# A decoder block on one core: the key numbers as sixteen steps, and most of the choice's conversions on ScalarE

## The chip, the cores and the metric

The kernel runs on one core of a Trainium2 chip. The metric is the device time of one execution in microseconds (us); the median of several runs is compared. The engines are named as the profile names them: PE is TensorE's matrix unit, PEld its weight loads, ACT is ScalarE, DVE is VectorE, POOL is GpSimd, and SP is the engine that issues most transfers.

## The reference, cut to what matters

The block mixes 512 tokens (an RWKV group and a sliding-window attention group) and then passes them through a channel mixer that retrieves experts by product keys. Only this last part touches the change. Each of 8 heads scores a token against two sets of 128 subkeys; the 16 best of each set are kept, their sums are ranked, the 16 best pairs are chosen, and each pair names one of 16384 experts:

```python
q = (x_b @ wq).reshape(-1, H, 2, PEER_HALF)
s = jnp.einsum('thcd,hcnd->thcn', q, subkeys)
s_top, i_top = lax.top_k(s, K)                       # K = 16
cand_s = s_top[:, :, 0, :, None] + s_top[:, :, 1, None, :]
cand_i = i_top[:, :, 0, :, None] * 128 + i_top[:, :, 1, None, :]
best_s, best_pos = lax.top_k(cand_s.reshape(-1, H, K * K), K)
idx = jnp.take_along_axis(cand_i.reshape(-1, H, K * K), best_pos, axis=-1)
gate = jax.nn.softmax(best_s, axis=-1)
u = u_tab[idx]
act = gelu(einsum('td,ted->te', x_b, u))
y = einsum('te,ted->td', gate * act, v_tab[idx])
```

## The kernel before

After the mixers the program has three stages that matter here. In the **selection stage** a loop (`for hc in range(16)`) makes the scores of one half-head a pass and ranks them. In the **gate stage** that follows, DVE builds one-hot tables of the chosen experts, PE multiplies them into a dense table of gates, and POOL gathers rows for 128 tokens. In the **main loop** over 128 blocks of experts PE does the dense products.

One pass of the selection loop is called a slot here, by its `hc` (slot 4, slot 5, ...). The order on each engine is the order of the code, since the whole stage is scheduled by hand (`manual_schedule` over POOL, DVE, ACT, PE and SP). A slot issues:

- `wq_split(hc + 1)`: ACT rounds the next slot's projection weights (`wqh`, L166), POOL makes their remainder (`wql`, L167);
- PE: the query product `pq` (24 matmuls, L176 to L178; every third one uses `wql`), and ACT copies it to `q`;
- two steps of work ahead for the main loop (`ups`): ACT rounds expert weights (`uh`), POOL makes `ul` (DVE does so for the later blocks), PE multiplies them (`pA`), ACT applies GELU (`act`);
- one step of the pending choice (`todo`);
- PE: the scores `psc` from `q` and the subkeys; ACT copies them to `sc`; DVE ranks them (`top`: five groups of MAX8, FIND_INDEX8 and MATCH_REPLACE8);
- one more step of the pending choice.

After four slots a set of eight (head, token tile) rows is ranked, and `choose` is started for it; its steps are spread over the next four slots. With the slots counted from the start of a set's choice (4, 5, 6, 7 for the first set):

- slot 4, first step: `fi` (the key numbers as floats), their differences `df` and the candidate sums `cand` on POOL; second step: DVE ranks half of `cand`;
- slot 5, second step: DVE ranks the other half into `bp`, then `ex`, `pf` (the positions as floats) and the first pair of comparisons `ge` against the offsets of the 16 candidate rows;
- slot 6, first step: POOL multiplies the pair `ge` by `df`; second step: DVE sums them into `ro`, adds the first key number, converts and splits the position (`bp`, `rn`, `ro`, `pf`), and makes the second pair `ge`;
- slot 7, first step: POOL multiplies that pair; second step: DVE sums it, ACT takes the exponential of `ex`, and the results go to `sg_`.

Three sets run so (`h0` of 0, 2 and 4, slots 4 to 15). The fourth (`h0 == 6`) runs after the loop with all its arithmetic on DVE, beside products ahead on PE, and the gate stage starts from its results.

Of the kernel before, what the change touches and what calls it, by code (L numbers as in the profile page):

```python
# [7 lines left out]
F32 = mybir.dt.float32  # L8
# [5 lines left out]
OP = mybir.AluOpType  # L14
# [8 lines left out]
TOPK = 16  # L23
# [31 lines left out]
OFFS = [sum(NCAND[:a]) for a in range(16)]  # L55
# [15 lines left out]
def peer_block_kernel(tc, A, out, dbg=None, stop=None):  # L71
    with ExitStack() as ctx:
        _emit(ctx, tc, A, out, dbg or {}, stop)


def _emit(ctx, tc, A, out, dbg, stop):
    nc = tc.nc
    V, SC, PE, GP, SY = nc.vector, nc.scalar, nc.tensor, nc.gpsimd, nc.sync
# [57 lines left out]
    for lv in range(5):  # L136
        b = 1 << lv
        n = 32 // (2 * b)
        for q in range(4):
# [6 lines left out]
                             base=0, channel_multiplier=1)  # L146
            GP.affine_select(out=m[:, :, b:2 * b], in_=m[:, :, b:2 * b],
                             pattern=[[2 * b, n], [0, b]], compare_op=OP.is_ge, fill=0.0,
                             base=b - 1, channel_multiplier=-1)
# [632 lines left out]
    iota = mp.tile([128, 128], F32, name="iota")  # L782
# [212 lines left out]
    sg_ = selp.tile([128, 3, NT, 8, TOPK], F32, name="sg_")  # L995
    tk = tkst.enter_context(tc.tile_pool(name="tk", bufs=1, side="right", reuse_waits="tile"))
    subk = tk.tile([128, 16, 128], F32, name="subk")
    SY.dma_start(subk, A["subk"])

    offs = tk.tile([128, 2, 15], F32, name="offs")  # L1000
    for a in range(1, 16):
        GP.memset(offs[:, 0, a - 1:a], float(OFFS[a]))
        GP.memset(offs[:, 1, a - 1:a], 128.0 * (OFFS[a] - OFFS[a - 1]))
    B815 = [128, 4, TOPK, 15]

    def top(rows):

        for v_, _, x in rows:
            V.max(v_[:, 0:8], x)
        for v_, i_, x in rows:  # L1010
            V.max_index(i_[:, 0:8], v_[:, 0:8], x)
        for v_, _, x in rows:
            V.match_replace(x, v_[:, 0:8], x, LOWEST)
        for v_, _, x in rows:
            V.max(v_[:, 8:16], x)
        for v_, i_, x in rows:
            V.max_index(i_[:, 8:16], v_[:, 8:16], x)

    def choose(h0, tv, ti):

        E_ = GP if h0 < 6 else V
        fi = tk.tile([128, 2, 8, TOPK], F32, name="fi", tag="fi", bufs=2)
        V.tensor_copy(fi, ti)
        df = tk.tile([128, 2, 8, 15], F32, name="df", tag="df", bufs=2)
        E_.tensor_tensor(out=df, in0=fi[:, :, :, 1:16], in1=fi[:, :, :, 0:15], op=OP.subtract)
        E_.tensor_tensor(out=df[:, 0], in0=df[:, 0], in1=offs[:, 1, None, :].to_broadcast([128, 8, 15]), op=OP.add)
        cand = tk.tile([128, 8, NC_], F32, name="cand", tag="cand", bufs=2)
        s1, s2 = tv[:, 0], tv[:, 1]
        for a in range(8):
            n = NCAND[a]  # L1030
            E_.tensor_tensor(out=cand[:, :, OFFS[a]:OFFS[a] + n], in0=s1[:, :, a:a + 1].to_broadcast([128, 8, n]),
                             in1=s2[:, :, 0:n], op=OP.add)
        E_.tensor_tensor(out=cand[:, :, OFFS[8]:], in0=s1[:, :, 8:16], in1=s2[:, :, 0:1].to_broadcast([128, 8, 8]),
                         op=OP.add)
        yield
        bv_ = tk.tile([128, 8, TOPK], F32, name="bv", tag="bv", bufs=2)
        bp = tk.tile([128, 8, TOPK], U32, name="bp", tag="bp", bufs=2)
        for hh in range(2):
            top([(bv_[:, g], bp[:, g], cand[:, g, :]) for g in range(4 * hh, 4 * hh + 4)])
            if hh == 0:  # L1040
                yield
                yield

        gs = tk.tile([128, 8], F32, name="gs", tag="gs", bufs=2)
        ex = tk.tile([128, 8, TOPK], F32, name="ex", tag="ex", bufs=2)
        V.tensor_tensor(out=ex, in0=bv_, in1=bv_[:, :, 0:1].to_broadcast([128, 8, TOPK]), op=OP.subtract)

        if h0 == 6:
            SC.activation(ex, ex, AF.Exp)
        pf = tk.tile([128, 8, TOPK], F32, name="pf", tag="pf", bufs=2)  # L1050
        V.tensor_copy(pf, bp)
        ro = tk.tile([128, 8, TOPK], F32, name="ro", tag="ro", bufs=2)
        rn = tk.tile([128, 8, TOPK], U32, name="rn", tag="rn", bufs=2)

        def pick(src, steps, base, dst):

            ges = []
            for hh in range(2):
                hs = slice(4 * hh, 4 * hh + 4)
                ge = tk.tile(B815, F32, name="ge", tag="ge", bufs=2)  # L1060
                V.tensor_tensor(out=ge, in0=src[:, hs, :, None].to_broadcast(B815),
                                in1=steps[:, None, None, :].to_broadcast(B815), op=OP.is_ge)
                ges.append(ge)
            yield
            for hh in range(2):
                hs = slice(4 * hh, 4 * hh + 4)
                E_.tensor_tensor(out=ges[hh], in0=ges[hh],
                                                    in1=df[:, base, hs, None, :].to_broadcast(B815), op=OP.mult)
            yield
            for hh in range(2):  # L1070
                hs = slice(4 * hh, 4 * hh + 4)
                V.tensor_reduce(dst(hh), ges[hh], axis=AX.X, op=OP.add)
                V.tensor_tensor(out=dst(hh), in0=dst(hh), in1=fi[:, base, hs, 0:1].to_broadcast([128, 4, TOPK]),
                                op=OP.add)


        yield from pick(pf, offs[:, 0, :], 0, lambda hh: ro[:, 4 * hh:4 * hh + 4])
        V.tensor_copy(bp, ro)
        V.tensor_scalar(rn, bp, 7, None, op0=OP.logical_shift_right)
        V.tensor_scalar(bp, bp, 127, None, op0=OP.bitwise_and)  # L1080
        V.tensor_copy(ro, rn)
        V.tensor_tensor(out=pf, in0=pf, in1=ro, op=OP.subtract)
        yield from pick(pf, iota[:, 1:16], 1, lambda hh: sg_[:, 2, :, h0 + hh, :])
        if h0 < 6:
            SC.activation(ex, ex, AF.Exp)
        HT = [128, 2, NT, TOPK]

        def by_tile(i):
            return sg_[:, i, :, h0:h0 + 2, :].rearrange("p t h s -> p h t s")

        def by_head(x):
            return x.rearrange("p (h t) s -> p h t s", t=NT)

        V.tensor_copy(by_tile(1), by_head(bp))
        V.tensor_reduce(gs, ex, axis=AX.X, op=OP.add)
        V.reciprocal(gs, gs)
        V.tensor_tensor(out=by_tile(0), in0=by_head(ex),
                        in1=gs.rearrange("p (h t) -> p h t", t=NT)[:, :, :, None].to_broadcast(HT), op=OP.mult)
# [12 lines left out]
    for hc in range(16):  # L1111
        h_, c_h = hc // 2, hc % 2
        if hc % 4 == 0:
            tv = tk.tile([128, 2, 8, TOPK], F32, name="tv", tag="tv", bufs=2)
            ti = tk.tile([128, 2, 8, TOPK], U32, name="ti", tag="ti", bufs=2)
# [25 lines left out]
        if hc % 4 == 3:  # L1141
            todo = choose(h_ - 1, tv, ti)
# [17 lines left out]
    tk = tkst.enter_context(tc.tile_pool(name="oh", bufs=1, side="right", reuse_waits="tile"))  # L1160
# [327 lines left out]
```

## Time and profile before

| | us |
|---|---|
| median of 3 runs | 1629.78 (1628.6 to 1633.54) |
| the profiled execution | 1630.73, of which span 1629.0 |
| PE busy | 1572.6 (97%) |
| DVE busy | 1286.1 (79%) |
| ACT busy | 652.5 (40%) |
| POOL busy | 742.4 (46%) |

The shares are means over stages with different limits, so the stage around the change has to be read by itself. The selection stage with the fourth set lies between about 374 and 579 us of the span, the gate stage between 579 and about 840 us. What a stage costs is read from which engine waits there, and for whom.

### The profile page before, as it was taken

The page shows a single profiled execution, that of the slowest core. Times are in us where ns is not written, and L with a number is a line of the kernel's source. Part 1 is how long each engine was busy: PE and PEld are TensorE (multiplying, and loading weights), DVE is VectorE, ACT ScalarE, POOL GpSimd, SP SyncE. Part 2 cuts the span into 40 slices and gives each one's busy share as a digit, 9 for nine tenths or more (in the row PEclk, how much of TensorE's full clock was granted, in tenths as well). Part 3 has the DMA queues.
Part 4 walks back from the last instruction along what each step waited for, and adds up shares of the span by engine and source line. Part 5 has one row for each costly group of instructions (what it writes and reads, how often), then busy time and mean ns, then how long its engine had stood idle before and what let it go on. Part 6 is the DMA issues. An engine that isn't in the chain of part 4 may idle for free.

```text
span 1629.0 us, 30768 instructions
## 1 busy us (share of the span) xinstructions
PE 1572.6 (97%) x11869; PEld 1366.7 (84%) x11869; DVE 1286.1 (79%) x2497; ACT 652.5 (40%) x1092; POOL 742.4 (46%) x711
## 2 busy tenths in 40 slices
PE   7999999899999889999999999999999999999997
PEld 4777777797999888888988888888888888888886
DVE  6666567756899999999677788777878877887896
ACT  5333345544444344454433333333333333333334
POOL 5121123244676512222155555555655556556582
PEclk9999999999999999999999999999999999999999
DMA  4111110333232269999999888889998988989793
GB/s 143 53 42 42 59 48 2 129 124 103 79 104 91 98 214 336 348 323 354 320 345 351 304 309 320 322 299 316 331 308 301 333 312 303 321 303 339 236 311 136
DMA packets 180548, 371.18 MB, mean 228 GB/s; under 512 B 17840, under 2 KB 102320, under 8 KB 180144
## 3 DMA queue, kind: packets, MB, share of 16 engines
q1 hardware_dynamic: 137488, 226.71, 40.6%
q0 software_dynamic: 36864, 134.23, 22.9%
q10 hardware_dynamic: 6048, 8.26, 1.4%
q8 instruction: 93, 1.52, 0.4%
q14 instruction: 55, 0.45, 0.1%
HBM read 333.62 MB, written 35.52 MB: 227 GB/s over the span
## 4 chain that ended last, share of the span: by engine, by line
PE 50%; DVE 11%; DMA 3%; issue 1%; ACT 1%; POOL 1%; SPq 0%; DVEq 0%; ACTq 0%
PE acc L1359 10%; PE acc L1358 10%; PE acc L1357 10%; PE pA L178 7%; PE pA L176 7%; PE pA L177 7%; DVE O L1228 3%; DVE ul L167 2%; DVE scr L1182 2%; DVE P L1233 2%; DMA u<-in_uT_dram 2%; DMA row<-in_vB_dram,ix 1%; DMA v<-in_vB_dram 0%; PE pG L1255 0%; POOL row L1169 0%
## 5 line engine op out<-in xcount | busy, mean ns | idle before, releaser
L178 PE MATMUL pA<-h2hi,ul 128*128 128x384 f32 x1024 | 346.2, 338 | 9.9 <-DVE ul L167 5.6
L176 PE MATMUL pA<-h2hi,uh 128*128 128x384 f32 x1024 | 350.3, 342 | 1.5 <-ACT actd L969 1.5
L177 PE MATMUL pA<-h2lo,uh 128*128 128x384 f32 x1024 | 344.1, 336 | 0.0
L1169 POOL DMA_INDIRECT row<-in_u_dram,ix x128 | 175.2, 1369 | 285.7 <-DVE scr L1182 247.7
L1359 PE MATMUL acc<-vl,wh 128*128 128x512 f32 x768 | 300.3, 391 | 1.5 <-DVE vl L167 1.5
L1358 PE MATMUL acc<-vh,wl 128*128 128x512 f32 x768 | 300.0, 391 | 0.2 <-DVE wl L167 0.2
L1357 PE MATMUL acc<-vh,wh 128*128 128x512 f32 x768 | 298.9, 389 | 1.3 <-ACT vh L166 1.3
L1169 POOL DMA_INDIRECT row<-in_vB_dram,ix x128 | 196.1, 1532 | 141.1 <-DVE x L1180 115.7
L167 DVE TENSOR_TENSOR vl<-v,vh 128x1024 fp32r<-128x1024 f32 x128 | 213.9, 1672 | 35.2 <-ACT vh L166 34.4
L178 PEld LDWEIGHTS pA<-h2hi,ul 128*128 128x128 f32 x1024 | 192.8, 188 | 14.8 <-DVE ul L167 10.5
L176 PEld LDWEIGHTS pA<-h2hi,uh 128*128 128x128 f32 x1024 | 193.0, 188 | 4.7 <-ACT actd L969 1.6
L177 PEld LDWEIGHTS pA<-h2lo,uh 128*128 128x128 f32 x1024 | 193.2, 189 | 3.0
L1180 DVE SCALAR_TENSOR_TENSOR x<-row,ac,x 128x1024 f32<-128x1024 f32 x128 | 173.2, 1353 | 7.9 <-DMA row<-in_vB_dram,ix 6.0
L1359 PEld LDWEIGHTS acc<-vl,wh 128*128 128x128 f32 x768 | 144.1, 188 | 32.2 <-DVE vl L167 2.2
L1357 PEld LDWEIGHTS acc<-vh,wh 128*128 128x128 f32 x768 | 144.2, 188 | 30.0 <-ACT vh L166 1.6
L1358 PEld LDWEIGHTS acc<-vh,wl 128*128 128x128 f32 x768 | 144.1, 188 | 29.4 <-DVE wl L167 0.6
L1182 DVE SCALAR_TENSOR_TENSOR scr<-row,h2g 128x1024 f32<-128x1024 f32 x128 | 158.2, 1236 | 1.3
L166 ACT CAST uh<-u 128x1024 fp32r<-128x1024 f32 x128 | 133.9, 1046 | 62.2 <-PE pA L177 29.5
L167 DVE TENSOR_TENSOR ul<-u,uh 128x1024 fp32r<-128x1024 f32 x109 | 134.0, 1230 | 20.1 <-ACT uh L166 17.0
L166 ACT CAST vh<-v 128x1024 fp32r<-128x1024 f32 x128 | 134.0, 1048 | 0.3 <-DMA gts<-gates 0.3
L969 ACT ACTIVATE act<-pA 128x384 f32<-128x384 f32 x86 | 42.2, 491 | 131.6 <-PE pA L178 131.5
L1256 ACT ACTIVATE gst<-pG 128x512 f32<-128x512 f32 x96 | 55.8, 597 | 97.6 <-PE pG L1255 95.9
(725 smaller groups left out, 2621.0 us busy)
## 6 DMA issues: line engine op xcount, KB each, us to landing
u<-in_uT_dram SPq DMA_DIRECT2D x128, 512.0 KB, 6.4
v<-in_vB_dram SPq DMA_DIRECT2D x128, 512.0 KB, 5.9
gts<-gates SPq DMA_DIRECT2D x384, 64.0 KB, 4.5
gates<-gst SPq DMA_DIRECT2D x11, 2048.0 KB, 11.5
w<-in_w_in_dram SPq DMA_DIRECT2D x40, 256.0 KB, 2.8
wq<-in_wq_dram SPq DMA_DIRECT2D x16, 512.0 KB
acts<-actd ACTq DMA_DIRECT2D x42, 192.0 KB, 6.3
act<-acts SPq DMA_DIRECT2D x42, 192.0 KB, 7.5
```

Of the source, the lines that this page charges most:

```text
L166: (hi_eng or SC.copy)(dst_hi, src)
L167: (lo_eng or V).tensor_tensor(out=dst_lo, in0=src, in1=dst_hi.bitcast(F32), op=OP.subtract)
L176: mm(ps, whi[k][:, :m], ahi[:, k], start=k == 0, stop=False)
L177: mm(ps, whi[k][:, :m], alo[:, k], start=False, stop=False)
L178: mm(ps, wlo[k][:, :m], ahi[:, k], start=False, stop=k == KD - 1)
L1169: GP.indirect_dma_start(r_, None, A["vB"].rearrange("b p d -> (b p) d") if w_ else A["u"], bass.IndirectOffsetOnAxis(ap=ix[:, w_, jj:jj + ...
L1180: V.scalar_tensor_tensor(x2[:, 0, :], r_, ac[:, jj:jj + 1], x2[:, 0, :], op0=OP.mult, op1=OP.add)
L1182: V.scalar_tensor_tensor(scr, r_, 1.0, h2g, op0=OP.mult, op1=OP.mult, accum_out=ac[:, jj:jj + 1])
L1256: SC.activation(gst[:, :, :, t4 * 4:t4 * 4 + 4].rearrange("p n g t -> p (n g) t"), p.rearrange("p t e -> p e t"), AF.Copy, scale=1.0 / GS)
L1357: mm(o, wh[:, ts], vh[:, ds_], start=b == 0, stop=False)
L1358: mm(o, wl[:, ts], vh[:, ds_], start=False, stop=False)
L1359: mm(o, wh[:, ts], vl[:, ds_], start=False, stop=b == 127)
```

## The change

The steps that a position is compared with get a sixteenth, the first one, which every position reaches; its weight in `df` is the first key number itself. The sum over 16 steps then is the key number, and the addition after each sum goes. So `offs`, `df` and `ge` are 16 wide where they were 15, and one copy fills the new first column of `df`. Beside it, the five conversions between integers and floats in a set's choice go from DVE to ACT for the first three sets; the fourth set keeps them on DVE.

```diff
-    offs = tk.tile([128, 2, 15], F32, name="offs")
-    for a in range(1, 16):
+    offs = tk.tile([128, 2, 16], F32, name="offs")
+    for a in range(16):
...
-    B815 = [128, 4, TOPK, 15]
+    B816 = [128, 4, TOPK, 16]
...
         E_ = GP if h0 < 6 else V
+        convert = SC.copy if h0 < 6 else V.tensor_copy
         fi = tk.tile([128, 2, 8, TOPK], F32, name="fi", tag="fi", bufs=2)
-        V.tensor_copy(fi, ti)
-        df = tk.tile([128, 2, 8, 15], F32, name="df", tag="df", bufs=2)
-        E_.tensor_tensor(out=df, in0=fi[:, :, :, 1:16], in1=fi[:, :, :, 0:15], op=OP.subtract)
+        convert(fi, ti)
+        df = tk.tile([128, 2, 8, 16], F32, name="df", tag="df", bufs=2)
+        E_.tensor_copy(df[:, :, :, 0:1], fi[:, :, :, 0:1])
+        E_.tensor_tensor(out=df[:, :, :, 1:], in0=fi[:, :, :, 1:16], in1=fi[:, :, :, 0:15], op=OP.subtract)
...
-        V.tensor_copy(pf, bp)
+        convert(pf, bp)
...
             for hh in range(2):
-                hs = slice(4 * hh, 4 * hh + 4)
                 V.tensor_reduce(dst(hh), ges[hh], axis=AX.X, op=OP.add)
-                V.tensor_tensor(out=dst(hh), in0=dst(hh), in1=fi[:, base, hs, 0:1].to_broadcast([128, 4, TOPK]),
-                                op=OP.add)
...
-        V.tensor_copy(bp, ro)
+        convert(bp, ro)
         V.tensor_scalar(rn, bp, 7, None, op0=OP.logical_shift_right)
         V.tensor_scalar(bp, bp, 127, None, op0=OP.bitwise_and)
-        V.tensor_copy(ro, rn)
+        convert(ro, rn)
         V.tensor_tensor(out=pf, in0=pf, in1=ro, op=OP.subtract)
-        yield from pick(pf, iota[:, 1:16], 1, lambda hh: sg_[:, 2, :, h0 + hh, :])
+        yield from pick(pf, iota[:, 0:16], 1, lambda hh: sg_[:, 2, :, h0 + hh, :])
...
-        V.tensor_copy(by_tile(1), by_head(bp))
+        convert(by_tile(1), by_head(bp))
```

On ACT, from the copy of a set's second slot's scores (slot 13 in the third set) to the copy of the next slot's scores, this stood before:

```order
L1134 COPY sc<-psc 128x512
L166 CAST wqh<-wq 128x1024
L1127 COPY q<-pq 128x512
L166 CAST uh<-u 128x1024
L969 ACTIVATE act<-pA 128x384
```

From that score copy on, it now reads, up to the conversion after the next score copy:

```order
L1133 COPY sc<-psc 128x512
L1053 CAST pf<-bp 128x128
L166 CAST wqh<-wq 128x1024
L1126 COPY q<-pq 128x512
L166 CAST uh<-u 128x1024
L969 ACTIVATE act<-pA 128x384
L1133 COPY sc<-psc 128x512
L1077 CAST bp<-ro 128x128
```

The conversion `pf` now stands between the score copy and the next weights' rounding, and `bp` (with `ro` behind it) stands in the same place one slot later.

On DVE, in a set's third slot (slot 6), from the first sum to the second pair of comparisons, this stood before:

```order
L1072 TENSOR_REDUCE ro<-ge 128x64
L1073 TENSOR_TENSOR ro<-ro,fi 128x64
L1072 TENSOR_REDUCE ro<-ge 128x64
L1073 TENSOR_TENSOR ro<-ro,fi 128x64
L1078 CAST bp<-ro 128x128
L1079 TENSOR_SCALAR rn<-bp 128x128
L1080 TENSOR_SCALAR bp<-bp 128x128
L1081 CAST ro<-rn 128x128
L1082 TENSOR_TENSOR pf<-pf,ro 128x128
L1061 TENSOR_TENSOR ge<-pf,iota 128x960 x2
```

The same place now reads:

```order
L1073 TENSOR_REDUCE ro<-ge 128x64 x2
L1078 TENSOR_SCALAR rn<-bp 128x128
L1079 TENSOR_SCALAR bp<-bp 128x128
L1081 TENSOR_TENSOR pf<-pf,ro 128x128
L1063 TENSOR_TENSOR ge<-pf,iota 128x1024 x2
```

Two additions and two conversions have left DVE here; the conversions lie on ACT, between the same neighbours by their data.

## Rows read from the trace of the kernel before

**Rows 1.** Busy time by stretch: length, PE, PEld, DVE, ACT, POOL, clock, DMA, GB/s.

```profile
480.00:520.00 40.00, 40.00 (x214) 36.11 (x213) 39.59 (x201) 15.69 (x21) 29.67 (x22) 1.00 0.31 106
520.00:560.00 40.00, 36.20 (x201) 35.60 (x200) 36.34 (x154) 18.35 (x24) 25.18 (x11) 0.96 0.24 80
560.00:600.00 40.00, 34.36 (x234) 32.62 (x233) 36.13 (x56) 14.73 (x27) 5.25 (x4) 0.96 0.46 161
720.00:760.00 40.00, 37.66 (x303) 34.51 (x302) 39.31 (x59) 20.76 (x35) 9.18 (x8) 1.00 0.89 317
880.00:920.00 40.00, 40.00 (x199) 35.74 (x198) 31.26 (x41) 13.13 (x19) 23.09 (x17) 1.00 0.91 322
```

**Rows 2.** PE's waits, 374 to 600 us: total, times, longest.

```profile
PE pA L178 <- POOL ul L167: 3.8, 1, 3.8
```

**Rows 3.** Instruction groups by shape, 374 to 590 us: busy us, mean ns.

```profile
L1067 POOL TENSOR_TENSOR ge<-ge,df 128x960 f32<-128x960 f32 x12 | 29.7, 2491 | 11.5 <-DVE ge L1061 11.5
...
L1061 DVE TENSOR_TENSOR ge<-pf,iota 128x960 f32<-128x960 f32 x8 | 8.9, 1155 | 0.1
...
L1073 DVE TENSOR_TENSOR sg__5356<-sg__5356,fi 128x64 f32<-128x64 f32 x8 | 6.2, 775 | 0.3
...
L1085 ACT ACTIVATE ex<-ex 128x128 f32<-128x128 f32 x3 | 0.9, 311 | 0.0
...
L1051 DVE CAST pf<-bp 128x128 f32<-128x128 uint32 x4 | 0.9, 216 | 0.0
```

**Rows 4.** ACT in order of time, slots 5 to 7: start, duration, idle before.

```profile
420.38 0.59 ACT L1134 COPY sc<-psc 128x512 f32<-128x512 f32 x1 [1.75 <-issue]
...
431.45 1.05 ACT L166 CAST wqh<-wq 128x1024 fp32r<-128x1024 f32 x1
436.48 0.59 ACT L1127 COPY q<-pq 128x512 f32<-128x512 f32 x1 [3.99 <-PE pq L178]
...
441.55 0.59 ACT L1134 COPY sc<-psc 128x512 f32<-128x512 f32 x1 [1.71 <-issue]
```

**Rows 5.** DVE in order of time, from slot 5 on.

```profile
421.00 0.87 DVE L1009 MAX8 tv<-sc 128x8 f32<-128x128 f32 x4 [2.76 <-ACT sc L1134]
...
428.75 0.27 DVE L1046 TENSOR_TENSOR ex<-bv 128x128 f32<-128x128 f32 x1
...
429.19 4.28 DVE L1061 TENSOR_TENSOR ge<-pf,offs 128x960 f32<-128x960 f32 x2
433.40 0.86 DVE L1009 MAX8 tv<-sc 128x8 f32<-128x128 f32 x4
...
438.09 1.12 DVE L1072 TENSOR_REDUCE ro<-ge 128x64 f32<-128x960 f32 x1
...
463.35 0.86 DVE L1009 MAX8 tv<-sc 128x8 f32<-128x128 f32 x4
```

**Rows 6.** DVE in the fourth set, the row after its longest wait.

```profile
559.83 1.23 DVE L167 TENSOR_TENSOR ul<-u,uh 128x1024 fp32r<-128x1024 f32 x1 [3.15 <-ACT uh L166]
```

**Rows 7.** POOL in order of time, slots 6 and 7.

```profile
428.95 2.45 POOL L167 TENSOR_TENSOR ul<-u,uh 128x1024 fp32r<-128x1024 f32 x1 [4.54 <-ACT uh L166]
432.55 4.95 POOL L1067 TENSOR_TENSOR ge<-ge,df 128x960 f32<-128x960 f32 x2 [1.16 <-DVE ge L1061]
437.46 2.40 POOL L167 TENSOR_TENSOR wql<-wq,wqh 128x1024 fp32r<-128x1024 f32 x1
...
444.85 2.88 POOL L1067 TENSOR_TENSOR ge<-ge,df 128x960 f32<-128x960 f32 x1 [2.66 <-DVE ge L1061]
```

**Rows 8.** PE around the scores of slot 7.

```profile
440.42 1.05 PE L1132 MATMUL psc<-subk,q 128*128 128x128 f32 x8
441.23 0.48 PE L176 MATMUL pq<-h2hi,wqh 128*128 128x512 f32 x1
...
441.77 0.40 PE L178 MATMUL pq<-h2hi,wql 128*128 128x512 f32 x1
```

**Rows 9.** The six us behind PE's longest wait, columns as in rows 1.

```profile
536.00:542.00 6.00, 5.46 (x22) 5.46 (x23) 5.79 (x21) 0.00 (x0) 2.83 (x2) 0.72 0.54 178
```

More of the change, by code (lines that the diff above doesn't have):

```diff
@@ L998, in _emit @@
     SY.dma_start(subk, A["subk"])
-    offs = tk.tile([128, 2, 15], F32, name="offs")
-    for a in range(1, 16):
-        GP.memset(offs[:, 0, a - 1:a], float(OFFS[a]))
-        GP.memset(offs[:, 1, a - 1:a], 128.0 * (OFFS[a] - OFFS[a - 1]))
-    B815 = [128, 4, TOPK, 15]
+    offs = tk.tile([128, 2, 16], F32, name="offs")
+    for a in range(16):
+        GP.memset(offs[:, 0, a:a + 1], float(OFFS[a]))
+        GP.memset(offs[:, 1, a:a + 1], 128.0 * (OFFS[a] - OFFS[max(a - 1, 0)]))
+    B816 = [128, 4, TOPK, 16]
     def top(rows):
@@ L1021, in choose @@
         E_ = GP if h0 < 6 else V
+        convert = SC.copy if h0 < 6 else V.tensor_copy
         fi = tk.tile([128, 2, 8, TOPK], F32, name="fi", tag="fi", bufs=2)
-        V.tensor_copy(fi, ti)
-        df = tk.tile([128, 2, 8, 15], F32, name="df", tag="df", bufs=2)
-        E_.tensor_tensor(out=df, in0=fi[:, :, :, 1:16], in1=fi[:, :, :, 0:15], op=OP.subtract)
-        E_.tensor_tensor(out=df[:, 0], in0=df[:, 0], in1=offs[:, 1, None, :].to_broadcast([128, 8, 15]), op=OP.add)
+        convert(fi, ti)
+        df = tk.tile([128, 2, 8, 16], F32, name="df", tag="df", bufs=2)
+        E_.tensor_copy(df[:, :, :, 0:1], fi[:, :, :, 0:1])
+        E_.tensor_tensor(out=df[:, :, :, 1:], in0=fi[:, :, :, 1:16], in1=fi[:, :, :, 0:15], op=OP.subtract)
+        E_.tensor_tensor(out=df[:, 0], in0=df[:, 0], in1=offs[:, 1, None, :].to_broadcast([128, 8, 16]), op=OP.add)
         cand = tk.tile([128, 8, NC_], F32, name="cand", tag="cand", bufs=2)
@@ L1059, in pick @@
                 hs = slice(4 * hh, 4 * hh + 4)
-                ge = tk.tile(B815, F32, name="ge", tag="ge", bufs=2)
-                V.tensor_tensor(out=ge, in0=src[:, hs, :, None].to_broadcast(B815),
-                                in1=steps[:, None, None, :].to_broadcast(B815), op=OP.is_ge)
+                ge = tk.tile(B816, F32, name="ge", tag="ge", bufs=2)
+                V.tensor_tensor(out=ge, in0=src[:, hs, :, None].to_broadcast(B816),
+                                in1=steps[:, None, None, :].to_broadcast(B816), op=OP.is_ge)
                 ges.append(ge)
@@ L1067, in pick @@
                 E_.tensor_tensor(out=ges[hh], in0=ges[hh],
-                                                    in1=df[:, base, hs, None, :].to_broadcast(B815), op=OP.mult)
+                                                    in1=df[:, base, hs, None, :].to_broadcast(B816), op=OP.mult)
             yield
             for hh in range(2):
-                hs = slice(4 * hh, 4 * hh + 4)
                 V.tensor_reduce(dst(hh), ges[hh], axis=AX.X, op=OP.add)
-                V.tensor_tensor(out=dst(hh), in0=dst(hh), in1=fi[:, base, hs, 0:1].to_broadcast([128, 4, TOPK]),
-                                op=OP.add)
         yield from pick(pf, offs[:, 0, :], 0, lambda hh: ro[:, 4 * hh:4 * hh + 4])
-        V.tensor_copy(bp, ro)
+        convert(bp, ro)
         V.tensor_scalar(rn, bp, 7, None, op0=OP.logical_shift_right)
         V.tensor_scalar(bp, bp, 127, None, op0=OP.bitwise_and)
-        V.tensor_copy(ro, rn)
+        convert(ro, rn)
         V.tensor_tensor(out=pf, in0=pf, in1=ro, op=OP.subtract)
-        yield from pick(pf, iota[:, 1:16], 1, lambda hh: sg_[:, 2, :, h0 + hh, :])
+        yield from pick(pf, iota[:, 0:16], 1, lambda hh: sg_[:, 2, :, h0 + hh, :])
         if h0 < 6:
```

## The prediction

> **What bounds the kernel now.** I read the busy time by stretch first [rows 1]. From 880 us on PE is busy for the whole stretch. It is also busy for all of 480 to 520 us, in the selection stage, with DVE at 39.59 of 40 beside it: there both engines are full. A slot lasts 10.585 us (score copies at 420.38 and 441.55, two slots apart [rows 4]), and PE sets that. Between 520 and 600 us PE is idle for 3.80 + 5.64 = 9.4 us, and in the gate stage (720 to 760 us) it has 37.66 us of work against DVE's 39.31. So PE time that is lost before 520 us is lost for good, unless the 9.4 us of idle time can take it up; DVE time counts from 560 us on.
>
> The waits show PE's one long stop in the selection: 3.8 us for POOL's `ul` [rows 2]. In the six us behind it the granted clock averages 0.72 of 2.4 GHz, so part of them ran at the lower level of 1.2 GHz; 0.28 x 6 = 1.7 us are lost to that [rows 9].
>
> ACT's time line shows how much room it has: in every slot it stands idle 3.99 us before the `q` copy, waiting for PE's product [rows 4]. `q` ends at 436.48 + 0.59 = 437.07 and PE uses it for the scores at 440.42 [rows 8], so 3.35 us of delay on ACT would cost nothing. DVE's time line shows that the ranking of slot 5 starts at 421.00, after a wait for the score copy, and that of slot 9 at 463.35 [rows 5], which is 42.35 us or four slots later: DVE falls behind inside a set and has caught up with PE once a set.
>
> **The change, part by part.** *DVE's work.* Per set four additions go, at 0.775 us for those of the second choice [rows 3] and about the same for the first: 3.1 us. Five conversions of about 0.22 go in each of the first three sets: 1.1. Eight operations grow by a fifteenth of about 1.155: +0.6. That is 3.6 us less per set, 10.8 us in three sets. It is worth nothing as long as PE is full; where it could pay is below.
>
> *The fourth set.* It keeps its conversions, has twelve grown operations (+0.9), one small copy (0.2) and no additions. It runs after DVE's longest wait, 3.15 us for ACT's `uh`, which PE's pace sets [rows 6], or ahead of it, where that wait covers it. I take 0, ends -0.7 and +0.5.
>
> *POOL.* One small copy and a subtraction a set, hidden in the second half of slot 4 behind DVE's ranking; the products of `ge` grow by a fifteenth, and come in below.
>
> *ACT.* Five conversions of some 0.31 us (the exponential of the same shape [rows 3]) are 1.6 us a set, against 4 x 3.99 us of idle time. Their place costs more than their length. `pf` needs the end of DVE's ranking in slot 5, `bp` and `ro` need the sums in slot 6; until then everything behind them on ACT waits: the next `wqh`, the next `q`, `uh`, GELU and score copy, and through `wqh` POOL's `wql`, which PE needs.
>
> I work this out on the clock of the trace, first set.
> - *`pf`.* The score copy of slot 5 ends at 420.97; DVE is done with its ranking at 428.75, when `ex` starts [rows 5]. So ACT stands still for 7.8 us. `pf` ends at 429.1, `wqh` (1.05) at 430.1, `q` (0.59) at 430.65. PE wanted it at 440.42 - 10.585 = 429.83, so slot 6's scores come 0.8 us late. `wql` (2.40 on POOL [rows 7]) ends at 432.55; the first matmul that uses it stands 1.35 us behind the scores [rows 8], at 432.0: another 0.6.
> - *The comparisons.* Before, the pair `ge` took 4.28 us instead of two times 1.155, since the first one had to wait while POOL's `ul` ran from 428.95 to 431.40 [rows 5, 7]. Now it is the second one that meets `wql` (430.1 to 432.55): the pair ends at 433.75, and the ranking of slot 6 starts 0.35 us later than the 433.40 of before. It takes 4.69 (433.40 to 438.09): 438.45.
> - *The products.* On POOL `wql` and `ul` now lie ahead of them. `ul` can follow the second `ge` at 433.75 and ends at 436.1. The pair took 4.95, of which the first, beside a `ge`, took 2.88 in the same place a slot later, so one alone takes 2.07 [rows 7]; two grown ones take 4.4: 440.55. The second sum (1.2) ends at 441.8. The same with 4.95 grown to 5.3 gives 0.85 more, the upper end.
> - *`bp` and `ro`.* ACT has stood since the score copy of slot 6. `bp` 0.31, the shift 0.23 on DVE, `ro` 0.31: ACT is free at 442.7. `wqh` to 443.7, `q` to 444.2, scores at 444.25 instead of 440.42: **3.8 us late**, the 0.8 + 0.6 of before included. So PE stands still for about 2.4 us there.
> - *`wql` of slot 7.* POOL starts it at 443.8 or, if it has to let a `ge` end, at 444.3, and ends 446.2 to 446.7; the first matmul that uses it would stand at 445.6. I take +1.1, ends 0 and 1.3.
>
> **4.9 us for the first set.** In slots 8 and 9 DVE, now ahead of PE's scores, waits for the score copy instead; its gain is gone, and the second set starts with everything 4.9 us later: 4.9 again. In the third set slot 15 rounds no further weights, so `q` comes 1.0 us sooner and no `wql` is waited for: 2.8. Together 12.6 us; ends 3.5 + 3.5 + 2.5 = 9.5 and 6.0 + 6.0 + 3.7 = 15.7.
>
> Behind the loop POOL's `ul`, for which PE waits 3.8 us, stands behind the products of slot 15. These now end 2.8 us later in the set's own time, as late as PE itself is, so that stop stays as long as it was. DVE is only about 9 us late then, but must wait at the place of rows 6 for `uh`, which PE's pace sets. So DVE enters the last part, and the gate stage, 12.6 us late, and behind it nothing has room.
>
> **Sum.** 1630.73 (the profiled execution, 0.95 above the median) + 12.6 = 1643.3; against the median 1642.4. I say 1643.
>
> **Rivals.**
> 1. *The clock.* The three stops of about 2.4 us, each with a shorter one near it, are each followed by a slow stretch as the 3.8 us stop was: 3 x 1.7 = 5.1 more, 1648. For: rows 9. Against: only a longer stop shows it. The Trainium skill (TensorE: Matmul & The Clock Gate, HAM oscillation) says that a wait which comes back in every pass of a loop can bring back the slow clock each time; rows 9 show it once here, none shows it for stops this short.
> 2. *Taken up behind the loop.* The 9.4 us that PE idles between 520 and 600 us shrink by as much as PE is late, since DVE is less late: 12.6 - 9.4 = +3.2, 1634. For: DVE has 10.8 us less to do. Against: rows 2 and 6 show both waits hanging on a rounding that waits for PE.
> 3. *Faster: DVE's relief pays.* ACT reaches `pf` and `bp` so that they fit into its 3.99 us of idle time, and the products of slot 15 come early; then the 3.8 us stop goes with its 1.7 us of slow clock: -5.5, 1625. It decides if ACT's standstill stays under 3.35 us; the rows give 7.8 at `pf`. The Trainium skill (Perfetto Trace Analysis, Optimizing Scalar/DVE Operations) advises moving work from a saturated DVE to ScalarE, and by that rule the time would fall; rows 1 do show DVE full and ACT under half, but not the place in ACT's order.
> 4. *Half of it.* `wql` is never late and the products run faster beside the ranking: +6 to +9, 1638.
>
> **How the numbers follow.** A measurement of this kernel can tell about 0.3% (4.9 us) from no change. The forecast (9.5 to 15.7) has 0.55, the clock 0.17, half of it 0.08, taken up 0.12, faster 0.08. All but the last two are slower by over 0.3%: 0.80; taken up is within it: 0.12; faster 0.08. The likeliest case's own range is 1639 to 1646. The range given reaches to 1634, where all idle time is taken up, and to 1650, for the clock with a little more; outside it are the faster case and some tails.
>
> **What would show it.** Right: the longest waits of PE are its scores waiting for ACT's `q`, about 0.8 us three times and 2.4 us three times, and every third matmul of a product waiting for POOL's `wql`; ACT's wait for DVE at `pf` and `bp` is about 8 us or more, six times; the gate stage's first DVE instructions stand some 12 to 13 us later; the main loop is as long as before. Wrong: if `q` still waits for PE in slots 6 and 7; if the idle time behind slot 15 is gone; or if the clock falls in the slots, which would show as a granted clock below 1.00 between 430 and 530 us.

## The result and the profile after

The changed kernel takes 1642.92 us (median of 6 runs, 1640.07 to 1649.02), against 1631.57 us for the kernel before (6 runs beside it). The ratio is 1.0075, with a 95% interval from 1.0053 to 1.0096: 0.75% slower. The medians differ by 11.4 us. The profiled execution is the fastest of the six, 1640.07 us with a span of 1638.4 us; it is 9.3 us over the profiled execution of before.

PE's waits first, from 374 to 620 us: us in total, times, longest. Before, the scores waited there for `q` twice, 1.4 us together, ahead of slot 4 (these two are among the eight), and the one long stop was the 3.8 us of [rows 2].

```profile
PE psc L1131 <- ACT q L1126: 8.5, 8, 2.1
...
PE pA L178 <- POOL ul L167: 3.5, 2, 2.6
PE pq L178 <- POOL wql L167: 2.8, 5, 0.8
```

Two waits are new in the slots from 5 on: the scores wait for ACT's `q`, and the products for POOL's `wql`. PE in order of time shows where they stand (start, duration, and in brackets the idle time ahead and what ended it): the scores of slot 4, those of slots 6, 7 and 8 with the products behind them, then the scores of slot 15, what follows the loop, and the transposes of the selection.

```profile
407.13 1.05 PE L1131 MATMUL psc<-subk,q 128*128 128x128 f32 x8
...
429.20 1.16 PE L1131 MATMUL psc<-subk,q 128*128 128x128 f32 x8 [0.56 <-ACT q L1126]
...
431.27 0.50 PE L178 MATMUL pq<-h2hi,wql 128*128 128x512 f32 x1 [0.44 <-POOL wql L167]
...
442.99 1.16 PE L1131 MATMUL psc<-subk,q 128*128 128x128 f32 x8 [2.14 <-ACT q L1126]
...
445.37 0.50 PE L178 MATMUL pq<-h2hi,wql 128*128 128x512 f32 x1 [0.75 <-POOL wql L167]
...
454.80 1.05 PE L1131 MATMUL psc<-subk,q 128*128 128x128 f32 x8
...
537.35 1.16 PE L1131 MATMUL psc<-subk,q 128*128 128x128 f32 x8 [1.19 <-ACT q L1126]
...
541.84 0.44 PE L178 MATMUL pA<-h2hi,ul 128*128 128x384 f32 x1 [0.90 <-POOL ul L167]
...
548.85 0.45 PE L178 MATMUL pA<-h2hi,ul 128*128 128x384 f32 x1 [2.56 <-POOL ul L167]
...
588.39 0.55 PE L1200 MATMUL psT<-ident,sg__5356 128*128 128x128 f32 x3 [1.21 <-DVE sg__5356 L1096]
```

The same places in the kernel before, slots 4 and 15 and the transposes:

```profile
408.66 1.05 PE L1132 MATMUL psc<-subk,q 128*128 128x128 f32 x8
...
525.10 1.05 PE L1132 MATMUL psc<-subk,q 128*128 128x128 f32 x8
...
578.27 0.55 PE L1201 MATMUL psT<-ident,sg__5356 128*128 128x128 f32 x3 [1.60 <-DVE sg__5356 L1097]
```

The second set of the changed kernel shows the same four stops (0.57, 0.43, 2.13, 0.74), the third 0.56, 0.44 and 1.19. ACT in order of time shows why, in slots 5 to 7:

```profile
418.95 0.58 ACT L1133 COPY sc<-psc 128x512 f32<-128x512 f32 x1 [1.77 <-PE psc L1131]
427.42 0.30 ACT L1053 CAST pf<-bp 128x128 f32<-128x128 uint32 x1 [7.89 <-DVE bp L1017]
427.63 1.05 ACT L166 CAST wqh<-wq 128x1024 fp32r<-128x1024 f32 x1
428.58 0.57 ACT L1126 COPY q<-pq 128x512 f32<-128x512 f32 x1
...
440.62 0.30 ACT L1077 CAST bp<-ro 128x128 uint32<-128x128 f32 x1 [9.58 <-DVE ro L1073]
441.21 0.30 ACT L1080 CAST ro<-rn 128x128 f32<-128x128 uint32 x1 [0.29 <-DVE rn L1078]
441.42 1.04 ACT L166 CAST wqh<-wq 128x1024 fp32r<-128x1024 f32 x1
442.36 0.58 ACT L1126 COPY q<-pq 128x512 f32<-128x512 f32 x1
```

ACT stands 7.89 us for a conversion of 0.30, and `wqh` and `q` follow it without a gap. In [rows 4] `wqh` came directly behind the score copy, and `q` waited 3.99 us for PE; now PE waits for `q`.

The shift can be followed at the scores, against the kernel before ([rows 8] for slot 7). This execution's copy of slot 5's scores stands 1.43 us earlier (418.95 against 420.38 [rows 4]; its front part was that much quicker). Counted from there, those of slot 6 are 0.80 us late, of slot 7 4.00, of slot 9 5.32, of slot 13 10.62, of slot 15 13.7. The selection's transposes behind the loop are 11.55 late, the end 10.8. So the loop lost 13.7, and 2.9 came back behind it.

The busy time by stretch (columns as in [rows 1]):

```profile
480.00:520.00 40.00, 37.12 (x190) 32.35 (x189) 33.65 (x176) 14.40 (x22) 30.52 (x23) 1.00 0.33 118
520.00:560.00 40.00, 34.35 (x189) 31.65 (x188) 36.79 (x186) 16.64 (x25) 27.66 (x11) 1.00 0.20 66
560.00:600.00 40.00, 34.93 (x215) 33.59 (x214) 36.70 (x45) 14.53 (x24) 11.35 (x7) 0.96 0.49 163
```

PE had 40.00 of 40 in 480 to 520 us and DVE 39.59; now PE has 37.12 and DVE 33.65. The clock is 1.00 from 520 to 560 us, where it was 0.96: the 3.8 us stop has become two of 0.90 and 2.56, and no slow clock follows either.

### The profile page after: what moved, and what is told of

The parts are those of the page before. It is cut to its first block, busy times and chain, and to the rows that moved or that the text cites. A ratio compares the mean times of both kernels' runs of the same rounds, so it can differ in the third digit from the quotient of the medians.

```text
span 1638.4 us, 30751 instructions
## 1 busy us (share of the span) xinstructions
PE 1576.1 (96%) x11869; PEld 1365.5 (83%) x11869; DVE 1283.4 (78%) x2467; ACT 654.6 (40%) x1107; POOL 746.3 (46%) x716
## 4 chain that ended last, share of the span: by engine, by line
PE 73%; DVE 13%; issue 5%; POOL 4%; DMA 3%; ACT 2%; SPq 1%; DVEq 0%; POOLq 0%; ACTq 0%
PE acc L1358 10%; PE acc L1357 10%; PE acc L1356 10%; PE pA L178 7%; PE pA L176 7%; PE pA L177 7%; PE pj L176 3%; PE pj L178 3%; PE pj L177 3%; DVE O L1227 3%; DVE scr L1181 2%; DVE ul L167 2%; DVE P L1232 2%; PE pq L178 1%; POOL wql L167 1%
```

## The experiments

The theory (A) was that the place of the conversions in ACT's order costs the time: ACT works its instructions off in order, and `wqh`, `q` and what PE needs of them stand behind a conversion that waits for DVE. Its rivals: the sixteenth step's wider operations cost it (B); the length of the work or the handing over between engines costs it, wherever it stands (C). Each kernel ran beside the kernel before on the same chip, whose median was 1631.35 us in the first four runs, 1631.98 in the next four and 1631.95 in the last three. The table gives for each the median, the ratio with its interval (estimated from all runs, so not quite the quotient of the two medians), and from its trace the distance from the scores of slot 4 to those of slot 15 (eleven slots; 116.44 us before, 130.22 in the changed kernel).

| kernel | median us | ratio, 95% interval | slots 4 to 15, us |
|---|---|---|---|
| sixteen steps alone | 1635.79 | 1.0020, 1.0008 to 1.0031 | 119.15 |
| the same, and unused ACT work without a wait | 1633.42 | 1.0014, 1.0003 to 1.0026 | 119.19 |
| the same, and one-column ACT copies that wait | 1643.93 | 1.0071, 1.0052 to 1.0091 | 128.19 |
| of the changed kernel, `pf` on ACT, `bp` and `ro` on DVE | 1641.36 | 1.0055, 1.0038 to 1.0073 | 125.44 |
| `bp` and `ro` on ACT, `pf` on DVE | 1644.68 | 1.0068, 1.0051 to 1.0085 | 129.00 |
| conversions alone, fifteen steps | 1641.74 | 1.0061, 1.0045 to 1.0077 | 128.06 |
| the changed kernel, conversions later on ACT | 1634.34 | 1.0011, 0.9999 to 1.0022 | 118.81 |
| conversions alone, later on ACT | 1632.86 | 1.0002, 0.9990 to 1.0013 | 116.79 |
| before, arrays allocated sixteen wide | 1632.92 | 1.0006, 0.9996 to 1.0017 | 117.41 |
| before, the third set's second products on DVE | 1636.86 | 1.0024, 1.0014 to 1.0034 | 116.44 |
| before, low parts placed otherwise | 1632.44 | 1.0006, 0.9993 to 1.0019 | 116.43 |

**The sixteen steps alone.**

```diff
-        convert = SC.copy if h0 < 6 else V.tensor_copy
+        convert = V.tensor_copy
```

> The sixteen steps alone, all conversions back on DVE. Theory A (the place of the conversions on ScalarE holds up PE): no stop of PE before the scores and none for wql; DVE's shorter chain brings POOL's products of the last slot some 1.6 us forward, so the 3.8 us stop of PE shrinks and the slow clock behind it may go: 0 to 6 us faster than before, about 1628.5. Theory B (the wider steps and their products are what costs): 5 us or more slower than before.

It was 0.2% slower than before, not faster. Theory A keeps its main point (11.4 us became 4.4), but its belief in DVE's relief falls. The trace shows where the additions' time went. First DVE of the kernel before, an addition in the first set and one in the fourth, where POOL is idle; then DVE of this kernel at the place of the first; then POOL of this kernel at that time:

```profile
441.03 1.24 DVE L1073 TENSOR_TENSOR ro<-ro,fi 128x64 f32<-128x64 f32 x1
...
562.15 0.22 DVE L1073 TENSOR_TENSOR ro<-ro,fi 128x64 f32<-128x64 f32 x1
```

```profile
440.40 2.43 DVE L1077 CAST bp<-ro 128x128 uint32<-128x128 f32 x1
```

```profile
440.38 2.38 POOL L167 TENSOR_TENSOR ul<-u,uh 128x1024 fp32r<-128x1024 f32 x1
```

The addition of 64 columns takes 0.22 us with POOL idle; in the loop its 1.24 us were mostly a wait for POOL (the mean of 0.775 in [rows 3] mixes waiting and free ones). With the addition gone, the conversion behind it starts 0.02 us after POOL's `ul` and takes 2.43 us instead of 0.23: it ends when `ul` does. DVE comes to its next comparisons at 443.86, before at 443.55, and its busy time in the whole execution is 1289.6 us, 3.5 more than before. The Trainium skill (SBUF — State Buffer, Who interferes with whom) says that DVE and GpSimd share a pair of ports, that a DVE instruction with two inputs, or a cast in its fast mode, needs it while GpSimd reads, and that the one who comes second is blocked and not slowed. The trace agrees: 2.43 us beside `ul`, 0.23 without.

The rest is PE's: two new stops, and the old one longer.

```profile
453.22 0.50 PE L178 MATMUL pq<-h2hi,wql 128*128 128x512 f32 x1 [0.62 <-POOL wql L167]
...
539.43 0.69 PE L178 MATMUL pA<-h2hi,ul 128*128 128x384 f32 x1 [4.22 <-POOL ul L167]
```

POOL's grown products take 5.61 us a pair against 4.95 [rows 7], so `wql` behind them is late for the product behind the scores of slots 8 and 12, and `ul` behind the last pair is 0.4 us later than in [rows 2].

**Length without a wait, and a wait without length.** To the kernel above, the one adds three conversions a set on ACT that nobody reads and whose input is long there; the other adds two copies of a single column, also unused, of what DVE has just written, at the places of `pf` and of `bp`.

```diff
+        if h0 < 6:
+            SC.copy(dum, ti[:, 0])
...
+        if h0 < 6:
+            SC.copy(dum, ti[:, 0])
+            SC.copy(dum, ti[:, 0])
```

```diff
+        if h0 < 6:
+            SC.copy(dum[:, 0:1], bp[:, 7, 15:16])
...
+        if h0 < 6:
+            SC.copy(dum[:, 1:2], ro[:, 7, 15:16])
```

> Steps alone, with three extra conversions a set on ScalarE at the places of pf, bp and ro, of the same size, that read numbers which are long there and whose result nobody uses (their data adds nothing to the output). Theory A: ScalarE's idle time takes 0.3 to 0.6 us a slot, so the same time as the steps alone within 1 us. Theory C (their length or ScalarE's share): a few us over the steps alone.

> The sixteen steps with all conversions on DVE, as in the first experiment, and beside them two ACT copies of a single column per set, unused, at the places of pf and bp: one reads what the ranking has just written, one what the sums have just written. ACT so stands as long as with the real conversions, but DVE's work is that of the first experiment. Theory A (the place in ACT's row costs, by the wait): PE's stops of about 0.5 us and of 1.5 to 2 us in each set as in the changed kernel, 1639 to 1643 us. Theory C (the cost is in work, ACT's or DVE's, and not in the wait): as the first experiment, 1634 to 1636 us.

The length cost nothing (119.19 us for the eleven slots against 119.15; the medians, 1633.42 and 1635.79 us, have intervals that overlap). The wait alone took as long as the whole change: 1643.93 us, 12.0 over the kernel before and 0.9 above A's range. Its eleven slots take 128.19 us, 2.0 less than the changed kernel's, but a slot in which PE does not stop takes only 10.53 us here and 10.67 there, which accounts for 1.5 of the 2.0. ACT of the second kernel, in order of time, and then its PE:

```profile
430.61 0.19 ACT L1055 CAST dum<-bp 128x1 f32<-128x1 uint32 x1 [7.89 <-DVE bp L1017]
430.71 1.04 ACT L166 CAST wqh<-wq 128x1024 fp32r<-128x1024 f32 x1
431.66 0.57 ACT L1131 COPY q<-pq 128x512 f32<-128x512 f32 x1
```

```profile
432.29 1.16 PE L1136 MATMUL psc<-subk,q 128*128 128x128 f32 x8 [0.58 <-ACT q L1131]
...
445.43 1.16 PE L1136 MATMUL psc<-subk,q 128*128 128x128 f32 x8 [1.51 <-ACT q L1131]
```

A copy of one column, 0.19 us long, holds ACT for the same 7.89 us as `pf` did, and PE stops at the same scores as in the changed kernel, for 0.58 and 1.51 us (there 0.56 and 2.14). This rules out C as far as it speaks of length.

**The two places apart.** In the changed kernel, `bp` and `ro` back on DVE; or `pf` alone back on DVE.

```diff
-        convert(bp, ro)
+        V.tensor_copy(bp, ro)
...
-        convert(ro, rn)
+        V.tensor_copy(ro, rn)
```

```diff
-        convert(pf, bp)
+        V.tensor_copy(pf, bp)
```

> Sixteen steps; on ScalarE only fi, the last conversion and pf; bp and ro on DVE. Theory A: the trace after shows 0.56 + 0.44 us of PE stops a set behind pf, so about 3 us over the steps alone, 1631 to 1633. Theory C (each conversion on ScalarE costs alike, by its length and its handing over): three of five of the whole loss, about 1638.

> Sixteen steps; on ScalarE only fi, the last conversion, bp and ro; pf on DVE. Theory A: scores of a set's fourth slot about 2.9 us late and wql 1.1 more, a little less in the third set: 9 to 10 us over the steps alone, 1637 to 1640. Theory C: four of five of the whole loss, about 1641.

`pf` alone was expected to cost little, and its kernel takes 10 us more than the kernel before. Over the steps alone the two kernels take 5.6 us (forecast about 3) and 8.9 us (forecast 9 to 10) more, the changed kernel with both places some 7: the costs of the two places do not add up. In absolute times both lie above theory A's ranges, by 8.4 and 4.7 us, and C's figures are nearer, so these two do not decide between them. Beside its stops of 0.57 and 0.42 us it has a third one two slots later, in the first two sets:

```profile
455.72 0.50 PE L178 MATMUL pq<-h2hi,wql 128*128 128x512 f32 x1 [1.32 <-POOL wql L167]
```

With `bp` and `ro` on DVE, these wait for POOL there, the second comparisons and POOL's second products come late, and `wql` behind them. The other kernel has stops of 2.20, 2.21 and 1.26 us ahead of its fourth slots' scores, and here the slow clock appears. The first of these stops, then the busy time in the 12 us around it (columns as in [rows 1]):

```profile
444.36 1.16 PE L1131 MATMUL psc<-subk,q 128*128 128x128 f32 x8 [2.20 <-ACT q L1126]
```

```profile
440.00:444.00 4.00, 2.15 (x13) 1.83 (x11) 3.47 (x6) 1.72 (x4) 0.10 (x1) 1.00 0.00 0
444.00:448.00 4.00, 3.04 (x13) 2.26 (x14) 4.00 (x4) 3.97 (x8) 4.00 (x2) 0.71 0.10 22
448.00:452.00 4.00, 4.00 (x10) 3.06 (x10) 4.00 (x29) 0.89 (x1) 4.00 (x2) 0.50 0.64 241
```

PE idled 2.20 us ahead of 444.36, and from 444 us on the granted clock averages 0.71, then 0.50, the level of 1.2 GHz. Behind the second set's stop it fell again, to 0.68 from 492 to 496 us and 0.89 from 496 to 500. Reckoned as for [rows 9], these slow stretches cost 3.2 and 1.7 us, so some 5 us of this kernel's 129.00 are the clock's. In the changed kernel's profile a stop of 2.14 us brought none. So stops of this length can bring the lower clock and need not. The Trainium skill's remark (TensorE: Matmul & The Clock Gate, HAM oscillation) that a wait in each pass of a loop can bring the slow clock back agrees with this execution, not with that one. The changed kernel's runs spread over 9 us: three of 1640.07 to 1642.15 us have a mean granted clock of 0.996, three of 1643.69 to 1649.02 us one of 0.991 to 0.993. That some had this slow stretch would fit, but only one of them was profiled, and the six of the kernel before, which has no such stop in its slots, spread over 7 us as well.

**The conversions alone**, on ACT in the kernel before, with fifteen steps and the additions.

```diff
+        convert = SC.copy if h0 < 6 else V.tensor_copy
-        V.tensor_copy(pf, bp)
+        convert(pf, bp)
```

(the other four likewise)

> The kernel before with its fifteen steps and its additions, and only the five conversions of the first three sets on ACT. Theory A (the conversions' place on ACT costs, the sixteenth step does nothing): as slow as the changed kernel or up to 3 us slower, 1641 to 1646 us. Rival (the sixteenth step's wider arrays carry a part of the loss, as the first experiment's 0.2% lets one think): 2 to 4 us below the changed kernel, 1637 to 1640 us.

1641.74 us, 1.0061: within what A expected, at its lower edge. The sixteenth step is not needed for the loss, so B explains at most a small part of it.

**The same operations, later on ACT.** This is the test that takes away the cause and leaves the work. The second step of slots 5 and 6, which holds the waiting conversions but no work of POOL or PE, is written later: that of slot 5 behind the next slot's `wqh` and `q`, that of slot 6 also behind its `uh` and GELU. DVE's and POOL's orders stay.

```diff
             SC.copy(q, p)
+        if hc > 4 and hc % 4 == 2:
+            steps(todo, 1)
         steps(ups, UPS1[hc])
+        if hc > 4 and hc % 4 == 3:
+            steps(todo, 1)
         steps(todo, 1)
...
-        steps(todo, 1)
+        if hc < 4 or hc % 4 in (0, 3):
+            steps(todo, 1)
```

> The changed kernel with every one of its operations, and only their place in ACT's row changed: pf's conversion is written behind wqh and q of the next slot, bp's and ro's behind wqh, q and the up product's uh and act as well. DVE's and POOL's rows keep their order. Theory A (what costs is what stands behind the waiting conversion): PE's stops of 0.56, 0.44, 2.14 and 0.75 us per set vanish or shrink below 0.5 us in all, and the time is that of the first experiment, 1633 to 1637 us. Rival (the handing over between DVE and ACT costs wherever it stands, for instance because DVE then waits for ACT and is late with its rankings): 1639 to 1643 us.

> The kernel before with fifteen steps and its additions, the five conversions of the first three sets on ACT, at the later places of the experiment above. Theory A: no stops in the loop, 1630 to 1633 us, the time of before, since DVE's relief is worth nothing while PE is full there. Rival (DVE's relief pays once nothing is held on ACT): 1625 to 1629 us.

The changed kernel's work in this order takes 1634.34 us, 2.4 us over the kernel before instead of 11.4. What is left is no more than the sixteen steps alone cost. Its ACT in order of time:

```profile
426.23 0.59 ACT L1126 COPY q<-pq 128x512 f32<-128x512 f32 x1 [4.07 <-PE pq L178]
429.11 0.30 ACT L1053 CAST pf<-bp 128x128 f32<-128x128 uint32 x1 [2.29 <-DVE bp L1017]
429.31 1.05 ACT L166 CAST uh<-u 128x1024 fp32r<-128x1024 f32 x1
...
436.90 0.59 ACT L1126 COPY q<-pq 128x512 f32<-128x512 f32 x1 [4.07 <-PE pq L178]
...
441.02 0.30 ACT L1077 CAST bp<-ro 128x128 uint32<-128x128 f32 x1 [0.77 <-DVE ro L1073]
443.43 0.30 ACT L1080 CAST ro<-rn 128x128 f32<-128x128 uint32 x1 [2.11 <-DVE rn L1078]
443.64 0.58 ACT L1137 COPY sc<-psc 128x512 f32<-128x512 f32 x1
```

`q` again waits for PE (4.07 us, as 3.99 in [rows 4]), and `pf` waits behind it, 2.29 us. No score waits for `q` in slots 4 to 15 any more. What is still to be seen in the slots are two stops for `wql`, of 0.44 and 0.42 us, at the same places as in the sixteen steps alone (0.62 each). The score copy of slot 7, at 443.64 behind `ro`, stands 2.81 us behind its scores (440.83) where it was 1.13 [rows 4, 8], and PE does not wait for it. This decides between A and C: the hand-over from DVE to ACT is all there, and free.

With fifteen steps and this order the time is that of before (1.0002). Five conversions a set less on DVE gave nothing: while PE is full, DVE's relief has no worth, as predicted. The advice of the Trainium skill (Perfetto Trace Analysis, Optimizing Scalar/DVE Operations) to take work from a full DVE to ScalarE so costs 0.6% here in the one order and brings nothing in the other.

**Sizes alone.** Before, with `offs`, `df` and `ge` allocated sixteen wide and one column unused, so that only places in SBUF change, and the stride of the rows of `offs` and `df`.

```diff
-        df = tk.tile([128, 2, 8, 15], F32, name="df", tag="df", bufs=2)
+        df = tk.tile([128, 2, 8, 16], F32, name="df", tag="df", bufs=2)[:, :, :, 0:15]
```

(`offs` and `ge` likewise)

> The kernel before, with the arrays of the steps' comparisons allocated sixteen wide and one column left unused, so that only the places of what is allocated behind them change. If the longer slot of the runs so far (10.67 us against 10.585) comes from where the weights' tiles stand: slots of 10.67 us again and about 1 us slower than before, 1632.5 us. Rival (it comes from the sixteen-wide work beside it): slots of 10.585 us and the time of before.

Its PE at the scores of two slots:

```profile
440.16 1.05 PE L1133 MATMUL psc<-subk,q 128*128 128x128 f32 x8
...
450.83 1.05 PE L1133 MATMUL psc<-subk,q 128*128 128x128 f32 x8
```

A slot lasts 10.67 us, as in the changed kernel, where it was 10.585: 0.97 us in eleven slots, with the same instructions in number and size. In the time itself it can't be told from nothing (1.0006, 0.9996 to 1.0017).

**Two tries at what bounds the kernel before.** Its stop of 3.8 us [rows 2] stands behind the last products on POOL. The first try puts the third set's second products on DVE; the second writes the low part of up block 14 ahead of the products, and gives POOL four low parts that DVE does behind the loop.

```diff
-                E_.tensor_tensor(out=ges[hh], in0=ges[hh],
+                (V if h0 == 4 and base == 1 else E_).tensor_tensor(out=ges[hh], in0=ges[hh],
```

```diff
-        split(uh, ul, us.pop(b), lo_eng=GP if 0 < b < 20 else V)
+        split(uh, ul, us.pop(b), lo_eng=GP if 0 < b < 23 or b == 24 else V)
...
+        if hc == 15:
+            up_split(14)
```

> The kernel before with one operation moved: the second comparison of the third set's pair, which stood on POOL, on DVE. Theory A (POOL's lateness in the last slot makes PE's stop of 3.8 us and the slow clock behind it): the stop before pA goes or shrinks below 1 us, no slow clock behind it, 1 to 4 us faster than before, 1628 to 1630 us. Rival (DVE then is late with something PE waits for): no change, 1631 to 1633 us.

> The kernel before without any of the change, and with two edits where the experiments place its own waits: the low part of up block 14 is written ahead of the last slot's products on POOL (it stood behind them, and PE stopped 3.8 us for it), and the low parts of blocks 20, 21, 22 and 24 behind the loop go from DVE to POOL (they took 4.8 us of DVE there and made it wait 5.0). If these two rows set the stretch from the loop's end to the selection: the stop of 3.8 us goes, the slow clock behind it too, and the selection begins 4 to 7 us earlier, 1624 to 1628 us. Rival (POOL then is late with the up blocks behind the loop, or what is won is waited for again ahead of the gates): 1629 to 1633 us.

Neither was faster. The first, at 1636.86 us, is slower than even its rival (1631 to 1633); that stop was gone, and another came. Its PE, then its ACT:

```profile
556.36 0.69 PE L176 MATMUL pA<-h2hi,uh 128*128 128x384 f32 x1 [6.80 <-ACT act L969]
```

```profile
553.26 0.31 ACT L1049 ACTIVATE ex<-ex 128x128 f32<-128x128 f32 x1 [9.38 <-DVE ex L1046]
```

DVE, some 4 us later, comes late to the fourth set's `ex`; ACT stands 9.38 us for it (0.96 before), with `uh` and GELU behind it. That is the changed kernel's mechanism at another place. The second lies in its rival's range: the stop shrank to 1.00 us, but another of 2.30 for GELU came later, and DVE lost beside POOL what it had handed over. DVE's two product pairs of the fourth set, in the kernel before and then in this one:

```profile
552.25 4.43 DVE L1067 TENSOR_TENSOR ge<-ge,df 128x960 f32<-128x960 f32 x2
...
569.39 2.22 DVE L1067 TENSOR_TENSOR ge<-ge,df 128x960 f32<-128x960 f32 x2
```

```profile
551.65 6.57 DVE L1067 TENSOR_TENSOR ge<-ge,df 128x960 f32<-128x960 f32 x2
...
566.51 6.64 DVE L1067 TENSOR_TENSOR ge<-ge,df 128x960 f32<-128x960 f32 x2
```

They take 6.56 us more, against 4.8 us of low parts given away. No kernel of this study beats the one before.

## Why the prediction was right

It said 1643.0 us; the median is 1642.92, inside the likeliest case's own range. The mechanism was right, but that the number fits to 0.1 us is luck: the loop lost 1.1 us more than forecast, 2.9 us that were not forecast came back behind it, and the single runs lie up to 6 us from their median. By its steps:

- **`pf`.** Forecast: ACT stands 7.8 us, scores of slot 6 are 0.8 late, the product behind them another 0.6. Measured 7.89, 0.80, and a stop of 0.44. Right.
- **`bp` and `ro`.** Forecast: the scores of slot 7 are 3.8 late with a stop of about 2.4. Measured 4.00 and 2.14. Right; the forecast left out what a stop costs beside its idle time. In an unbroken product the matmuls last 0.40 us and start 0.23 us apart (at 431.61, 431.84 and 432.07 in this trace), so they overlap by 0.17; at a stop this overlap is lost, and the first matmul behind it takes 0.50 us (scores 1.16 instead of 1.05). That makes some 0.28 us a stop, and the four stops of a set (3.89 us idle) make its slots 5.0 us longer.
- **`wql` behind the scores of slot 7.** Forecast 1.1, measured 0.75.
- **Per set and in all.** 4.9 forecast, 5.3 measured, of which 0.34 is the longer slot (4 x 0.085) that the sizes alone show and that no step had. The third set 2.8, measured 3.06. In all 12.6 forecast; the loop lost 13.7, the end 10.8.
- **Behind the loop.** "That stop stays as long as it was" was wrong in form: 3.80 us became 0.90 + 2.56, and the slow clock behind it, 1.7 us [rows 9], went. 2.1 us came back there by the selection's transposes, and 0.7 later. Most of the 2.1 is the slow clock, which the forecast had gone only in its third rival. Of the second rival little came true: PE's stops from the scores of slot 15 to the transposes shrank from 6.2 us to 5.3.
- **DVE's work.** Forecast 3.6 us less a set, 10.8 in all, and worth nothing. It is worth nothing (the later order shows that), but its size was wrong: DVE's busy time falls only from 1286.1 to 1283.4 us. Most of the 0.775 us of an addition was a wait for POOL that the profile counts as busy, and it moves to another instruction: in the steps alone to the conversion behind it, in the changed kernel in part to the second comparisons (1.76 us each instead of 1.155). The additions of the fourth set, 0.22 us each, could have told.
- **The clock** (first rival, +5.1). Not in the changed kernel's profile, but in that of the kernel with `bp` and `ro` on ACT, behind stops of 2.20 and 2.21 us. Stops of 2.14 and 2.13 us did not bring it.
- **Sixteen steps at no cost.** They were expected to be free; alone they cost 0.2%: late `wql` in two slots, a longer `ul` stop, and about 1 us from the slots of 10.67 us that come with the wider arrays.

Shown by the experiments: the wait ahead of `wqh` and `q` in ACT's order is the cause, since a wait without the work brings the loss, and the same work, waiting where nothing that PE needs soon stands behind it, does not. Open: what makes the clock fall behind one stop of 2.2 us and not behind another, and how often it did in the unprofiled runs.

## What to carry to other kernels

Before an operation is given to an engine with idle time, look at what stands behind it in that engine's order and at when its input is ready: the price is that wait less the slack of the work behind it, not its own duration. The same offload was free here a few instructions later, behind the work that another engine waits for. And a short operation with a long duration in the profile, beside a busy neighbour, can be a wait that will move, not work that will go.

## What the runs showed of the hardware

- With the same instructions, a slot of PE took 10.67 us instead of 10.585 when three arrays were allocated one column wider. In the traces every kernel with the narrow arrays has 10.58 to 10.59, and every one with the wide ones 10.67, but for the kernel with the small unused tiles, which has 10.53. Where nothing but the sizes changed, only the places of tiles in SBUF and the row stride of two arrays differ; that small tiles moved the pace again speaks for the places. By which tile, no run here tells.
- DVE's small conversions (0.23 us) took up to 2.43 us beside one POOL instruction that had started 0.02 us earlier, and the profile counts the wait as busy time. Sums (reductions) of 1024 columns beside POOL's `wql` kept their 1.2 us each (2.32 for two in the steps alone, 2.34 in the fourth set).
- Behind a stop of 2.20 us the granted clock was 0.50 from 448 to 452 us in one execution; behind stops of 2.14 and 2.56 us it stayed at 1.00 in another. The stop of 2.57 us behind the loop of the first, at the same place as the other's 2.56, was followed by 0.64 from 552 to 556 us.
- A stop of PE cost some 0.28 us more than its idle time: four stops of 3.89 us made the slots of a set 5.0 us longer.
